# Weight-block sums stored ahead for v and the last gate; the last stage's rows kept in operand tiles, its norm's weights applied before the root

## The chip, the cores and the metric

One Trainium2 chip, one NeuronCore of it. The metric is device time in microseconds of one execution, the median of three runs. All engine times below come from one profiled execution, in which each engine's instructions are recorded; times there count from the start of the span.

## The reference, cut to what matters

A decoder layer on h of shape (1024 tokens, 1024 channels), float32. The parts that the change touches are the projection for v and the last step:

```python
z = rmsnorm(h, mix_pre_g) @ w_in          # 1024 x 5120; columns 1024:2048 are v
v = gelu(z[..., 1024:2048])               # then a layer norm and the spatial gate
...
gate = sigmoid(rmsnorm(h, ple_pre_g) @ ple_w_gate)
e = p @ ple_w_proj
h = h + rmsnorm(gate * e, ple_post_g)     # rmsnorm(y, g) = y * rsqrt(mean(y*y) + 1e-6) * g
```

Ahead of each of the two products stands a feed-forward block, h + 0.5 * rmsnorm((silu(n @ w_gate) * (n @ w_up)) @ w_down), with 2816 hidden channels.

## The kernel before, in words

Every large product is made from seven products of half-sized blocks (a Winograd form of Strassen's scheme). `ORDER` lists them as p1, p2, p5, p6, p3, p7, p4. A float32 operand is split in two float32r parts, high and low: `split` (L147, L148) makes a cast on ScalarE (ACT) and a subtraction on VectorE (DVE). `mm3` (L155 to L157) makes three matmuls of 128x512 from them.

The left operand's seven sums live in seven tiles of the pool X (class `Seven`, one [128, 2, 4, 512] tile for each product; the pool has seven buffers, and an eighth tile, `rest`, holds sums in between). They are made from the normed rows of eight token tiles t = 0 to 7. `closing` computes such a row tile when the product before it ends: the residual (L730), its squares on ACT (L168), the root on GpSimd (POOL; `rsqrt`, L162 and L163), the norm (`scaled`, L178), then `feed`: eight transposes on TensorE (PE; L232) and the sums and splits of the transposed tile (L207, L212, L214, L215, L148). Tiles 4 to 7 come last, and their `late` part feeds p5 and what follows.

The right operand of v and of the last gate is made by class `Rows`: two half tiles (pool wt, four buffers) for each of the seven products, one product ahead of its use. With no stored sums it takes `from_blocks`: p1 and p2 use a block as loaded, p5, p6, p7 and p4 add blocks in place with `each` (L368, recorded at L151), two additions of 128x1024 on DVE for each product. With stored sums (w_out_a, w_out_b and w_o already have them, by `store_sums` during the first feed-forward block's second product) it takes `from_stored`: p1, p2, p3 load a block, the other four load a sum from DRAM, and nothing is added.

`Rows.run` makes four products of 12 matmuls for each entry of `ORDER`, one for each of four row groups. Entry i takes t = 0 to 3; block results are combined by `Out.read` (L333 to L345) and handed to `final`: half 0 of tiles 0 to 3 at p2, half 1 of them at p3, half 1 of tiles 4 to 7 at p7 and half 0 at p4. For v that is `v_final`, for the last stage `ple_final` (L1169): a load of e's half row into a tile of pool hf (four buffers), sigmoid (L1179), the product with e (L1180), squares (L168) and a part of the mean on POOL (L174). A tile's second half also loads h's row into a tile of pool raw (six buffers, shared with the weight loads), takes the root, and for each half scales (L178), adds the row (L151) and stores (L1191).

`Later` holds deferred steps with a key and a cost in us; `allow` pops some after each product, `flush` empties it. In `ffn_hidden` (two calls, 11 groups of columns each) `after(c)` defers the group's sums (`spill`) and `down_sums(c)`, which for one 128-row pair of w_down loads two tiles of pool f (11 buffers), makes four additions of 128x512 and stores four results. All loads and stores but four go through SyncE's (SP's) queue in order. The order on each engine comes from a list scheduler that simulates the program; the program's order is the priority.

Of the kernel before, what the change touches and what calls it, by code (L numbers as in the profile page):

```python
# [8 lines left out]
F32 = mybir.dt.float32  # L9
FR = mybir.dt.float32r  # L10
AF = mybir.ActivationFunctionType
ALU = mybir.AluOpType
# [71 lines left out]
def layer_kernel(ctx: ExitStack, tc: tile.TileContext, a: dict, out: bass.AP):  # L84
# [42 lines left out]
    def scratch(name, n, w=D):  # L127
        return [dr.tile([P, w], F32, name=f"{name}{i}", tag=f"{name}{i}") for i in range(n)]
# [4 lines left out]
    as_d, bs_d = (scratch(s, 7, KD // 2 * HT) for s in ("a_s", "b_s"))  # L133

    tw_d = {s: [scratch(f"{s}_t{h}", 4) for h in range(2)] for s in ("w_out_a", "w_out_b", "w_o")}
    ws_d = dr.tile([P, HT], F32, name="ws_d", tag="ws_d")
# [43 lines left out]
    def gain(vec):  # L180
        g = full()
        nc.sync.dma_start(g, vec.partition_broadcast(P))
        return g
# [5 lines left out]
    class Seven:  # L189
        def __init__(self):  # L190
            self.op, self.kept = [None] * 7, {}
            count[0] += 10
            self.base = count[0]
# [312 lines left out]
    class Rows:  # L506
        def __init__(self, w, stored=None):

# [24 lines left out]

            make = from_stored(block, put, sums) if stored else from_blocks(block, put)
            self.right = Right(lambda i: make(i, state, (False, False)), list(range(7)), 1)

        def run(self, left, outs, last):
            for i, (name, place, fresh) in enumerate(ORDER):
                if i == 6:
                    last()  # L540
                left.need(i)
                o = self.right.get(i)
                for t in range(4):
                    if i == 2:
# [45 lines left out]

    def ffn_hidden(s, left, cols, last):
        wd = a[f"{s}_w_down"][0]
# [38 lines left out]
        def after(c):  # L631
            spill(hid.pop(c), lambda i: s_d[s][i][:, c * HT:(c + 1) * HT])
            if c < HC - 1:
                down_sums(c)
            if c == HC - 2:
                down_sums(c + 1)
            if c == HC - 1:
                later.flush()
# [233 lines left out]

    down = down_weights("ffn1")
    ffn_hidden("ffn1", left, h1_cols, lambda: down.ahead(3))
    v_rows = Rows(w_in[:, D:2 * D])
    left = Seven()
# [279 lines left out]

    down = down_weights("ffn2")
    ffn_hidden("ffn2", left, h2_cols, lambda: down.ahead(3))
    ple_rows = Rows(a["ple_w_gate"][0])
    left = Seven()  # L1160
# [5 lines left out]

    m, parts, gains = {}, {}, []

    def ple_final(t, half_, part):  # L1169
        if not gains:  # L1170
            gains.append(gain(a["ple_post_g"][0]))
        g_ple = gains[0]
        h = slice(half_ * HT, (half_ + 1) * HT)
        if t not in m:
            m[t] = full()
        mt = m[t]
        e = half()
        nc.sync.dma_start(e, e_d[t][:, h])
        nc.scalar.activation(mt[:, h], part, AF.Sigmoid)  # L1179
        nc.vector.tensor_tensor(mt[:, h], mt[:, h], e, op=ALU.mult)  # L1180
        if half_ != (1 if t < 4 else 0):
            parts[t] = mean_part(mt[:, h], e, 1.0 / D, EPS)
            return
        hp = raw([D])
        nc.sync.dma_start(hp, h3_d[t])
        r = rsqrt(squares(mt[:, h], e), 1.0 / D, parts[t])
        for j in range(2):
            hj = slice(j * HT, (j + 1) * HT)
            scaled(mt[:, hj], mt[:, hj], r, g_ple[:, hj])
            add(hp[:, hj], hp[:, hj], mt[:, hj])  # L1190
            nc.sync.dma_start(out[0, t * P:(t + 1) * P, hj], hp[:, hj])  # L1191

    ple_rows.run(left, token_out(ple_final, m), lambda: None)


# [27 lines left out]
```

## Time and profile before

| what | us |
|---|---|
| median of 3 runs | 2148.37 (2146.13 to 2148.41) |
| the profiled execution | 2153.78 |
| its span, first to last instruction | 2151.7 |
| mean granted TensorE clock | 0.983 of full speed |
| PE busy | 2070.9 (96%) |
| DVE busy | 1472.0 (68%) |
| ACT busy | 939.9 (44%) |

Read the shares of busy time as averages over stages. The table of stretches gives the same for each stage, the timelines tell which instruction an idle engine waited for, in square brackets with the idle time ahead of it. A row that merges several instructions has xN at its end.

### The profile page before, as it was taken

Reading aid. Unit: us, or ns where it says so; the run is one execution under the profiler, and the core shown is the slowest. Engines: PE = TensorE matmul, PEld = TensorE weight load, DVE = VectorE, ACT = ScalarE, POOL = GpSimd, SP = SyncE. Lnnn points to the kernel's source line nnn. Section 1 sums busy time; section 2 is a strip of 40 time slices with the busy share of each in tenths; the row PEclk is TensorE's granted clock in tenths of the full one; section 3 lists DMA queues with packets and bytes.
Section 4 is the critical chain, followed back from the end, with each engine's and each line's share of the span. In section 5 each row is a group of like instructions: output and inputs, shape, how many; then the busy total and the mean of one; then the engine's idle time right before and its main releaser. Section 6 shows DMA issues by size and latency. Waiting matters only on the chain. (4 is left out here: it accounts for less than half of the span.)

```text
span 2151.7 us, 25497 instructions
## 1 busy us (share of the span) xinstructions
PE 2070.9 (96%) x9228; PEld 1712.7 (80%) x9228; DVE 1472.0 (68%) x1773; ACT 939.9 (44%) x1360; POOL 141.0 (7%) x212
## 2 busy tenths in 40 slices
PE   7999999999999799999999999989999999999986
PEld 6888888888887688888787887778888888888765
DVE  6866666677566887567576758886666667545687
ACT  7533333344435543334455535643333334444553
POOL 2000000000021110000000002300000000002112
PEclk9999999999999899999999999999999999999988
DMA  8454545399768236445389986635454547764635
GB/s 287 128 171 157 176 142 184 129 340 384 298 221 320 69 100 193 158 142 177 128 282 340 324 233 204 195 112 188 146 186 136 172 149 272 231 197 175 225 118 195
DMA packets 301486, 429.52 MB, mean 200 GB/s; under 512 B 19888, under 2 KB 176560, under 8 KB 301360
## 3 DMA queue, kind: packets, MB, share of 16 engines
q1 hardware_dynamic: 300272, 425.80, 58.3%
q0 software_dynamic: 1088, 2.10, 0.6%
q8 instruction: 72, 1.18, 0.2%
q14 instruction: 54, 0.44, 0.1%
HBM read 290.72 MB, written 137.10 MB: 199 GB/s over the span
## 5 line engine op out<-in xcount | busy, mean ns | idle before, releaser
L155 PE MATMUL ps<-X,wt 128*128 128x512 f32 x1904 | 743.0, 391 | 4.1 <-DVE f L345 2.4
L156 PE MATMUL ps<-X,wt 128*128 128x512 f32 x1904 | 743.2, 390 | 0.9 <-DVE X L148 0.9
L157 PE MATMUL ps<-X,wt 128*128 128x512 f32 x1904 | 741.8, 390 | 0.0
L148 DVE TENSOR_TENSOR wt<-raw,wt 128x1024 fp32r<-128x1024 f32 x282 | 343.5, 1220 | 235.0 <-ACT wt L147 234.9
L155 PEld LDWEIGHTS ps<-X,wt 128*128 128x128 f32 x1904 | 359.3, 189 | 79.3 <-DVE f L345 2.8
L156 PEld LDWEIGHTS ps<-X,wt 128*128 128x128 f32 x1904 | 359.2, 189 | 76.0 <-DVE X L148 1.8
L157 PEld LDWEIGHTS ps<-X,wt 128*128 128x128 f32 x1904 | 358.8, 188 | 74.7
L147 ACT CAST wt<-raw 128x1024 fp32r<-128x1024 f32 x282 | 295.5, 1050 | 268.7 <-PE ps L157 129.2
L148 DVE TENSOR_TENSOR X<-raw,X 128x1024 fp32r<-128x1024 f32 (+1 forms) x201 | 224.0, 1145 | 113.6 <-ACT X L147 113.1
L147 ACT CAST X<-raw 128x1024 fp32r<-128x1024 f32 (+1 forms) x201 | 192.1, 993 | 156.2 <-PE ps L157 66.6
L156 PE MATMUL ps<-X 128*128 128x512 f32 x616 | 241.5, 392 | 0.3 <-DVE X L148 0.3
L155 PE MATMUL ps<-X 128*128 128x512 f32 x616 | 237.4, 391 | 3.7 <-ACT X L147 2.6
L157 PE MATMUL ps<-X 128*128 128x512 f32 x616 | 240.2, 391 | 0.0
L151 DVE TENSOR_TENSOR raw<-raw 128x1024 f32<-128x1024 f32 x136 | 165.8, 1221 | 15.4 <-DMA raw<-in_w_in_dram 5.5
L155 PEld LDWEIGHTS ps<-X 128*128 128x128 f32 x616 | 116.1, 189 | 28.6 <-ACT X L147 3.0
L156 PEld LDWEIGHTS ps<-X 128*128 128x128 f32 x616 | 116.4, 189 | 24.7 <-DVE X L148 0.8
L156 PE MATMUL ps<-wt,X 128*128 128x512 f32 x336 | 133.8, 398 | 1.8 <-DVE wt L148 1.8
L157 PEld LDWEIGHTS ps<-X 128*128 128x128 f32 x616 | 116.4, 189 | 24.0
L155 PE MATMUL ps<-wt,X 128*128 128x512 f32 x336 | 132.1, 401 | 1.2 <-DVE f L345 1.2
L157 PE MATMUL ps<-wt,X 128*128 128x512 f32 x336 | 133.0, 396 | 0.0
L340 ACT ACTIVATE f<-ps 128x512 f32<-128x512 f32 x88 | 52.6, 598 | 122.5 <-PE ps L157 122.3
L338 ACT ACTIVATE f<-ps 128x512 f32<-128x512 f32 x88 | 52.0, 597 | 109.4 <-PE ps L157 109.4
(136 smaller groups left out, 1856.9 us busy)
## 6 DMA issues: line engine op xcount, KB each, us to landing
raw<-ffn_s SPq DMA_DIRECT2D x70, 512.0 KB, 5.2
raw<-in_ffn_w_gate_dram SPq DMA_DIRECT2D x96, 256.0 KB, 3.4
raw<-in_ffn_w_up_dram SPq DMA_DIRECT2D x96, 256.0 KB, 4.1
f<-in_ffn_w_down_dram SPq DMA_DIRECT2D x44, 512.0 KB, 4.6
ffn_s<-hf SPq DMA_DIRECT2D x88, 256.0 KB, 3.4
ffn_t<-hf SPq DMA_DIRECT2D x88, 256.0 KB, 4.3
raw<-ffn_t SPq DMA_DIRECT2D x40, 512.0 KB, 5.2
ffn_s<-f SPq DMA_DIRECT2D x66, 256.0 KB, 2.1
```

The costliest lines, as they stand in the source:

```text
L147: nc.scalar.copy(hi, src)
L148: e.tensor_tensor(lo, src, hi.bitcast(F32), op=ALU.subtract)
L151: e.tensor_tensor(dst, u, v, op=ALU.add)
L155: nc.tensor.matmul(ps, wl[1], wr[0], start=first, stop=False, skip_group_check=True)
L156: nc.tensor.matmul(ps, wl[0], wr[1], start=False, stop=False, skip_group_check=True)
L157: nc.tensor.matmul(ps, wl[0], wr[0], start=False, stop=last, skip_group_check=True)
L338: nc.scalar.activation(at("22"), y, AF.Copy, scale=-1.0)
L340: nc.scalar.activation(at("12"), x, AF.Copy, scale=-1.0)
```

## The change

The weight-block sums for v (columns 1024:2048 of w_in) and for ple_w_gate are made during the two `ffn_hidden` calls and stored in DRAM: after groups 3 to 6, `row_sums` defers a step (key 92) that loads two tiles of pool f (rows k and 512 + k of the matrix, 512 KB each) and, two products later, a step (key 93, cost 2.8) with four additions of 128x512 and four stores. `Rows` for v and for the last gate then always takes `from_stored`.

In the last stage e's rows and h's rows are loaded as whole rows, four to a tile of pool X: e's eight rows and the norm's weights at entry 3 (p6), h's rows 0 to 3 at entry 4 (p3) and 4 to 7 at entry 5 (p7). `ple_final` only applies the sigmoid at once; the rest is a step `gated`, kept in a list until its rows have been asked for. For p2's four halves that is the first call at p3. `gated` multiplies by e, takes the squares (the junk goes to a half tile), then multiplies by the norm's weights while the root is pending; after the root a fused multiply and add (mt * r + h) for each half replaces the scale and the addition.

```diff
--- before.py
+++ after.py
@@ -132,6 +132,7 @@
     ga_d, gb_d, y_d = (dr.tile([P, KD, T], F32, name=s, tag=s) for s in ("ga_d", "gb_d", "y_d"))
     as_d, bs_d = (scratch(s, 7, KD // 2 * HT) for s in ("a_s", "b_s"))
 
+    tr_d = {s: [scratch(f"{s}_t{h}", 4) for h in range(2)] for s in ("w_v", "ple_w_gate")}
     tw_d = {s: [scratch(f"{s}_t{h}", 4) for h in range(2)] for s in ("w_out_a", "w_out_b", "w_o")}
     ws_d = dr.tile([P, HT], F32, name="ws_d", tag="ws_d")
     sv_d = dr.tile([P, KD, T], F32, name="sv_d", tag="sv_d")
@@ -504,7 +505,7 @@
         return [one(t) for t in range(4)]
 
     class Rows:
-        def __init__(self, w, stored=None):
+        def __init__(self, w, stored):
 
             state = {}
 
@@ -531,15 +532,16 @@
                     out.append(o)
                 return out
 
-            make = from_stored(block, put, sums) if stored else from_blocks(block, put)
+            make = from_stored(block, put, sums)
             self.right = Right(lambda i: make(i, state, (False, False)), list(range(7)), 1)
 
-        def run(self, left, outs, last):
+        def run(self, left, outs, last, beside=lambda i: None):
             for i, (name, place, fresh) in enumerate(ORDER):
                 if i == 6:
                     last()
                 left.need(i)
                 o = self.right.get(i)
+                beside(i)
                 for t in range(4):
                     if i == 2:
                         later.flush(t + 6 if t < 3 else None)
@@ -588,7 +590,27 @@
         wg, wu = (a[f"{s}_w_{n}"][0] for n in ("gate", "up"))
         return Columns(HC, lambda c: ((wg, c, c + HC), (wu, c, c + HC)), 2)
 
-    def ffn_hidden(s, left, cols, last):
+    def row_sums(w, dst):
+
+
+        def one(k):
+            tiles = [full((2, HT)) for _ in range(2)]
+            for r, t in enumerate(tiles):
+                rows = w[r * HT + k * P:r * HT + (k + 1) * P, :]
+                nc.sync.dma_start(t, rows.rearrange("p (c f) -> p c f", c=2))
+
+            def sums():
+                b11, b12, b21, b22 = (t[:, c, :] for t in tiles for c in range(2))
+                for d, t, u, v in ((0, b11, b11, b12), (2, b12, b12, b22), (1, b22, b11, b22), (3, b21, b22, b21)):
+                    add(t, u, v)
+                    nc.sync.dma_start(dst[k // 2][d][:, (k % 2) * HT:(k % 2 + 1) * HT], t)
+
+            later.add(93, 2.8, sums, 2)
+
+        return [lambda k=k: later.add(92, 0.0, lambda: one(k)) for k in range(4)]
+
+    def ffn_hidden(s, left, cols, last, beside):
+
         wd = a[f"{s}_w_down"][0]
         hid = {}
 
@@ -630,6 +652,8 @@
 
         def after(c):
             spill(hid.pop(c), lambda i: s_d[s][i][:, c * HT:(c + 1) * HT])
+            if c > 2 and beside:
+                beside.pop(0)()
             if c < HC - 1:
                 down_sums(c)
             if c == HC - 2:
@@ -871,8 +895,8 @@
         return steps
 
     down = down_weights("ffn1")
-    ffn_hidden("ffn1", left, h1_cols, lambda: down.ahead(3))
-    v_rows = Rows(w_in[:, D:2 * D])
+    ffn_hidden("ffn1", left, h1_cols, lambda: down.ahead(3), row_sums(w_in[:, D:2 * D], tr_d["w_v"]))
+    v_rows = Rows(w_in[:, D:2 * D], tr_d["w_v"])
     left = Seven()
     ffn_down(
         down, closing(4.0, lambda t: x[t * P:(t + 1) * P, :], h1_d, "ffn1_post_g", "mix_pre_g", left),
@@ -1155,8 +1179,8 @@
     )
 
     down = down_weights("ffn2")
-    ffn_hidden("ffn2", left, h2_cols, lambda: down.ahead(3))
-    ple_rows = Rows(a["ple_w_gate"][0])
+    ffn_hidden("ffn2", left, h2_cols, lambda: down.ahead(3), row_sums(a["ple_w_gate"][0], tr_d["ple_w_gate"]))
+    ple_rows = Rows(a["ple_w_gate"][0], tr_d["ple_w_gate"])
     left = Seven()
     ffn_down(
         down, closing(4.0, lambda t: h2_d[t], h3_d, "ffn2_post_g", "ple_pre_g", left),
@@ -1164,33 +1188,50 @@
     )
 
 
-    m, parts, gains = {}, {}, []
+    m, parts, gains, e, h = {}, {}, [], {}, {}
+
+    def rows_of(src, dst, ts):
+        tile4 = X([4, D], F32)
+        for n, t in enumerate(ts):
+            dst[t] = tile4[:, n]
+            nc.sync.dma_start(dst[t], src[t])
+
+    def beside(i):
+        if i == 3:
+            gains.append(gain(a["ple_post_g"][0]))
+            rows_of(e_d, e, range(4))
+            rows_of(e_d, e, range(4, 8))
+        if i in (4, 5):
+            rows_of(h3_d, h, range(4 * i - 16, 4 * i - 12))
 
     def ple_final(t, half_, part):
-        if not gains:
-            gains.append(gain(a["ple_post_g"][0]))
-        g_ple = gains[0]
-        h = slice(half_ * HT, (half_ + 1) * HT)
+        cols = slice(half_ * HT, (half_ + 1) * HT)
         if t not in m:
             m[t] = full()
         mt = m[t]
-        e = half()
-        nc.sync.dma_start(e, e_d[t][:, h])
-        nc.scalar.activation(mt[:, h], part, AF.Sigmoid)
-        nc.vector.tensor_tensor(mt[:, h], mt[:, h], e, op=ALU.mult)
-        if half_ != (1 if t < 4 else 0):
-            parts[t] = mean_part(mt[:, h], e, 1.0 / D, EPS)
-            return
-        hp = raw([D])
-        nc.sync.dma_start(hp, h3_d[t])
-        r = rsqrt(squares(mt[:, h], e), 1.0 / D, parts[t])
-        for j in range(2):
-            hj = slice(j * HT, (j + 1) * HT)
-            scaled(mt[:, hj], mt[:, hj], r, g_ple[:, hj])
-            add(hp[:, hj], hp[:, hj], mt[:, hj])
-            nc.sync.dma_start(out[0, t * P:(t + 1) * P, hj], hp[:, hj])
-
-    ple_rows.run(left, token_out(ple_final, m), lambda: None)
+        nc.scalar.activation(mt[:, cols], part, AF.Sigmoid)
+
+        def gated():
+            nc.vector.tensor_tensor(mt[:, cols], mt[:, cols], e[t][:, cols], op=ALU.mult)
+            if half_ != (1 if t < 4 else 0):
+                parts[t] = mean_part(mt[:, cols], half(), 1.0 / D, EPS)
+            else:
+                r = rsqrt(squares(mt[:, cols], half()), 1.0 / D, parts[t])
+            nc.vector.tensor_tensor(mt[:, cols], mt[:, cols], gains[0][:, cols], op=ALU.mult)
+            if half_ != (1 if t < 4 else 0):
+                return
+            for j in range(2):
+                hj = slice(j * HT, (j + 1) * HT)
+                nc.vector.scalar_tensor_tensor(h[t][:, hj], mt[:, hj], r, h[t][:, hj], op0=ALU.mult, op1=ALU.add)
+                nc.sync.dma_start(out[0, t * P:(t + 1) * P, hj], h[t][:, hj])
+
+        gated_steps.append(gated)
+        if e and (t >= 4 or half_ == 0 or len(h) > t):
+            while gated_steps:
+                gated_steps.pop(0)()
+
+    gated_steps = []
+    ple_rows.run(left, token_out(ple_final, m), lambda: None, beside)
 
 
 # ---- launch: one core; inputs and outputs as the reference has them ----
```

## Rows read from the trace of the kernel before

**Rows 1.** From the page: the span, and each engine's busy us, share of the span and instructions.

```profile
span 2151.7 us, 25497 instructions
PE 2070.9 (96%) x9228; PEld 1712.7 (80%) x9228; DVE 1472.0 (68%) x1773; ACT 939.9 (44%) x1360; POOL 141.0 (7%) x212
```

**Rows 2.** The table of stretches: start and end, length, each engine's busy us (instructions), the granted TensorE clock, the DMA engines' mean share, GB/s. In order: most of the first hidden stage, v's stage, the hand-over into the last stage, the rest of its products, and the end.

```profile
60.00:465.00 405.00, 405.00 (x1788) 335.48 (x1787) 275.50 (x334) 152.38 (x202) 0.00 (x0) 1.00 0.51 170
...
690.00:771.00 81.00, 68.07 (x295) 55.69 (x295) 62.14 (x81) 42.23 (x70) 15.90 (x18) 0.92 0.25 79
...
2030.00:2075.00 45.00, 32.59 (x139) 26.08 (x138) 38.81 (x51) 25.44 (x48) 12.69 (x16) 0.85 0.41 141
2075.00:2134.00 59.00, 56.91 (x249) 46.24 (x247) 40.98 (x56) 29.46 (x54) 9.20 (x16) 1.00 0.52 164
2134.00:2151.70 17.70, 0.00 (x0) 0.00 (x0) 12.11 (x19) 2.65 (x7) 4.49 (x6) 0.62 0.36 137
```

**Rows 3.** The timeline of PE in the two hand-overs, the transposes of tiles 5, 6 and 7 alone: start, us, engine, line, operation, out<-in, count, and the idle time ahead with what ended it. First v's, then the last stage's.

```profile
702.57 1.09 PE L232 MATMUL ps<-ident,raw 128*128 128x128 f32 x8 [3.05 <-DVE raw L178]
...
711.71 1.97 PE L232 MATMUL ps<-ident,raw 128*128 128x128 f32 x8 [2.58 <-DVE raw L178]
...
726.45 1.97 PE L232 MATMUL ps<-ident,raw 128*128 128x128 f32 x8 [6.60 <-DVE raw L178]
...
2043.11 1.09 PE L232 MATMUL ps<-ident,raw 128*128 128x128 f32 x8 [1.96 <-DVE raw L178]
...
2052.26 1.27 PE L232 MATMUL ps<-ident,raw 128*128 128x128 f32 x8 [2.59 <-DVE raw L178]
...
2067.60 1.97 PE L232 MATMUL ps<-ident,raw 128*128 128x128 f32 x8 [7.17 <-DVE raw L178]
```

**Rows 4.** The timeline of DVE in the same two hand-overs: the weight additions (L151 raw<-raw 128x1024) and the norms of tiles 5, 6 and 7 (L178), some thirty other rows left out.

```profile
699.49 1.22 DVE L151 TENSOR_TENSOR raw<-raw 128x1024 f32<-128x1024 f32 x1 [4.10 <-DMA raw<-in_w_in_dram]
...
701.23 1.28 DVE L178 SCALAR_TENSOR_TENSOR raw<-f,sc 128x1024 f32<-128x1024 f32 x1
...
710.36 1.30 DVE L178 SCALAR_TENSOR_TENSOR raw<-f,sc 128x1024 f32<-128x1024 f32 x1 [0.72 <-POOL sc L163]
...
719.85 2.35 DVE L151 TENSOR_TENSOR raw<-raw 128x1024 f32<-128x1024 f32 x2
...
725.12 1.27 DVE L178 SCALAR_TENSOR_TENSOR raw<-f,sc 128x1024 f32<-128x1024 f32 x1
...
2040.03 1.23 DVE L151 TENSOR_TENSOR raw<-raw 128x1024 f32<-128x1024 f32 x1 [3.02 <-DMA raw<-in_ple_w_gate_dram]
...
2041.78 1.28 DVE L178 SCALAR_TENSOR_TENSOR raw<-f,sc 128x1024 f32<-128x1024 f32 x1
...
2048.37 1.22 DVE L151 TENSOR_TENSOR raw<-raw 128x1024 f32<-128x1024 f32 x1
...
2050.91 1.30 DVE L178 SCALAR_TENSOR_TENSOR raw<-f,sc 128x1024 f32<-128x1024 f32 x1 [0.72 <-POOL sc L163]
...
2061.01 1.21 DVE L151 TENSOR_TENSOR raw<-raw 128x1024 f32<-128x1024 f32 x1
...
2066.27 1.27 DVE L178 SCALAR_TENSOR_TENSOR raw<-f,sc 128x1024 f32<-128x1024 f32 x1
```

**Rows 5.** The timeline of POOL: the second instruction of tile 5's root in v's and in the last hand-over, the first instruction of tile 6's root in the last hand-over, and that of the first output tile's root at p3.

```profile
696.38 0.55 POOL L163 TENSOR_TENSOR sc<-sc,nhalf 128x1 f32<-128x1 f32 x1
...
2038.01 0.55 POOL L163 TENSOR_TENSOR sc<-sc,nhalf 128x1 f32<-128x1 f32 x1
...
2047.33 2.92 POOL L162 TENSOR_SCALAR sc<-sc 128x1 f32<-128x1 f32 x1 [7.10 <-ACT raw L168]
...
2104.51 0.26 POOL L162 TENSOR_SCALAR sc<-sc 128x1 f32<-128x1 f32 x1 [18.29 <-ACT hf L168]
```

**Rows 6.** The timelines of DVE and PE at the change from p7 to p4.

```profile
2116.51 1.23 DVE L151 TENSOR_TENSOR raw<-raw 128x1024 f32<-128x1024 f32 x1 [0.48 <-DMA raw<-in_ple_w_gate_dram]
...
2122.12 0.50 PE L155 MATMUL ps<-wt,X 128*128 128x512 f32 x1 [1.22 <-DVE f L345]
2123.26 0.49 PE L156 MATMUL ps<-wt,X 128*128 128x512 f32 x1 [0.63 <-DVE wt L148]
```

**Rows 7.** The timelines at the end: the sigmoid and the two scales of the first output tile at p3, then the last matmul, the wait for e, the last stores and the last additions.

```profile
2102.17 0.63 ACT L1179 ACTIVATE f<-f 128x512 f32<-128x512 f32 x1 [1.91 <-DVE f L342]
...
2105.44 1.41 DVE L178 SCALAR_TENSOR_TENSOR f<-f,sc 128x512 f32<-128x512 f32 x2 [0.58 <-POOL sc L163]
...
2133.38 0.39 PE L157 MATMUL ps<-wt,X 128*128 128x512 f32 x1
2135.25 0.69 DVE L1180 TENSOR_TENSOR f<-f,hf 128x512 f32<-128x512 f32 x1 [3.53 <-DMA hf<-e]
...
2141.04 7.87 SPq L1191 DMA_DIRECT2D out_dram<-raw  x8
...
2145.46 3.08 DVE L151 TENSOR_TENSOR raw<-raw,f 128x512 f32<-128x512 f32 x5
```

**Rows 8.** From the stretch 60 to 465 us (hidden stage): one line of its DMA issues (out<-in, queue, count, KB each, median us to landing) and the longest line of the SP queue's waits (us in total, times, longest us).

```profile
f<-in_ffn_w_down_dram SPq DMA_DIRECT2D x22, 512.0 KB, 4.7
...
SPq L563 <- DVE f L627: 141.6, 22, 13.8
```

**Rows 9.** The table of stretches, just after the last stage's last transposes (columns as in Rows 2).

```profile
2067.60:2073.40 5.80, 5.80 (x18) 4.92 (x19) 5.80 (x10) 4.37 (x10) 1.36 (x2) 0.50 0.43 140
```

## The prediction

> **What bounds the kernel now.** I began with the page. PE is busy for 96% of the span, DVE for 68%, ACT for 44% [rows 1]. So only time in which PE idles or runs slowly, and what follows its last matmul, can be won. The table of stretches says where that is [rows 2]. In the hidden stage PE is busy for all of its 405 us, 1788 matmuls at 0.2265 us; nothing can be won there, only lost. In v's stage PE lacks 12.9 of 81 us, in the hand-over into the last stage 12.4 of 45, in the rest of its products 2.1 of 59, and after 2134 us it does nothing for 17.7 us while DVE is busy for 12.1. These four places are where the change works, or can.
>
> PE's timeline in both hand-overs has the same picture: before the transposes of tiles 5, 6 and 7 it waits 3.05, 2.58 and 6.60 us in v's stage and 1.96, 2.59 and 7.17 us in the last, each time for the norm L178 on DVE [rows 3]. Between two sets of transposes stand only 24 matmuls, 24 x 0.2265 = 5.4 us and about 0.8 us for the transposes, while the norms of tiles 5, 6 and 7 follow each other in 9.13 and 14.76 us (v) and in 9.13 and 15.36 us (last) [rows 4]. So DVE's chain sets the pace of the hand-overs. Its rows show weight additions in it, L151 on raw tiles, and the first of them holds DVE, which takes its queue in order, for 4.10 us (v) and 3.02 us (last) while its weights come by DMA [rows 4].
>
> **Part 1: no weight additions in the hand-overs.** An addition costs 2.35 / 2 = 1.18 us [rows 4]. Four lie ahead of tile 7's norm in each hand-over: p5's two and p6's two.
>
> First additions: with them goes the wait. In the last stage DVE stops at 2040.03 - 3.02 = 2037.01; tile 5's root is out of POOL at 2038.01 + 0.55 = 2038.56 [rows 5], so its norm can start at some 2038.8 in place of 2041.78, 3.0 us earlier, not the whole 4.2. In v's stage the stop begins at 695.39, the root is out at 696.38 + 0.55 = 696.93 [rows 5], and the norm starts at some 697.1 in place of 701.23: 4.1 us. PE takes tile 5's transposes when its 24 matmuls are done, some 1 us after the norm; DVE runs on ahead, so what it won is not lost.
>
> Second addition: 1.2 us of the 9.13 us between tiles 5 and 6. POOL's small root operation took 2.92 us at 2047.33, against 0.26 us elsewhere [rows 5]; its record ends with the run of DVE instructions that the addition at 2048.37 lengthens. So root and DVE both come earlier by the one addition; it counts once, 1.2.
>
> Third and fourth: 2.35 us of the 14.76 and 15.36 us between tiles 6 and 7, 2.4. The sum: tile 7's transposes 4.1 + 1.2 + 2.4 = **7.7 us** earlier in v's stage, 3.0 + 1.2 + 2.4 = **6.6 us** earlier in the last. PE still has to wait for them: in v's stage tile 6's would be at 711.71 - 5.3 = 706.4, its work ends at about 713, and tile 7's come at 726.45 - 7.7 = 718.8. The whole 7.7 and 6.6 thus reach PE, and since it still idles some 6 us the clock drop behind it (granted 0.50, that is 1.2 GHz, for 5.8 us [rows 9]) stays as it is. From below, this part is worth nothing if another step of the chain (POOL, or the order) turns out to hold the norms; from above, the whole of the waits ahead of tiles 5 to 7, some 12 us in each stage.
>
> Stored sums need casts and subtractions as before; p5 now loads two tiles and not four. Six raw tiles suffice for p5's and the four rows of the residual, and its loads no longer wait for one to come free. Loaded bytes go up by one block of a megabyte in each stage, at 0.25 and 0.41 DMA share [rows 2]; nothing.
>
> At the change from p7 to p4 PE waits 1.22 + 0.63 us [rows 6]: a weight load that had waited for a raw tile, then an addition, cast and subtraction. Raw tiles no longer hold h's rows and the addition is gone: **1.9 us**.
>
> **Part 2: the end.** The last matmul ends at 2133.38 + 0.39 = 2133.8, the span at 2151.7: 17.9 us. DVE waits 3.53 us for e's row, which had no free tile of the four, and then works off a heap: the last five additions alone are 3.08 us, and eight stores follow each other [rows 7]. With e and h loaded ahead, what must follow the last matmul is one tile's chain. The first tile at p3 shows its length undisturbed: from its sigmoid at 2102.17 through product, squares and root to the end of two scales at 2105.44 + 1.41 = 2106.85, 4.7 us [rows 7]; the fused pair is taken at the price of the scales. From DVE's last end, 2145.46 + 3.08 = 2148.54, to the span's end are 3.2 us of store. That is 7.9 us.
>
> It needs DVE to keep up. A half-row operation costs 3.08 / 5 = 0.62 us [rows 7], an entry of `ORDER` 48 x 0.2265 = 10.9 us on PE. The change does not lower the count: six half operations for a tile before (two products with e, two scales, two additions), six after (two with e, two with the weights, two fused). p3 takes 20 of them with the four reads and two weight subtractions, 12.4 + 2.4 = 14.8 us; p7 12 and two, 9.8; p4 16, 9.9. From 34.5 us against 32.7 about 1.8 us are left over at the end. The four halves of p2 that now wait for e must fit into p6, where DVE is nearly idle (tile 7's sums and two subtractions); e's first tile can use the X buffer of p2's operand, free since p2's end, and the weight loads of p3 stand ahead of e's in SP's queue, those of p7 and p4 ahead of h's. I take 7.9 + 1.8 = 9.7 us in place of 17.9: **8.2 us**.
>
> Here a rule speaks against the change. The row shows what a run of DVE instructions does to POOL's root: 2.92 us and not 0.26 [rows 5]. At p4 all DVE work would be of that kind (the sums come straight from PSUM to ACT), and the product with the norm's weights is put exactly beside the root. The Trainium skill (SBUF — State Buffer, "Who interferes with whom") says that a Vector instruction with two SBUF inputs and a GpSimd instruction that reads SBUF exclude each other for a whole instruction; the row agrees in kind, though the wait spans several instructions. The product is queued while ACT still takes the squares, so I count no wait on the last tile; by the row it would be 2.92 - 0.26 = 2.7 us, which a rival takes up.
>
> **Part 3: what is added.** Eight steps of `row_sums`, each two loads of 512 KB, four additions of 128x512 (2.5 us at 0.62) and four stores, in the hidden stages. The nearest rows are `down_sums`' own: 22 such loads (eleven steps) in a stretch in which PE lost nothing and DVE had 405 - 275.5 = 129 us free, ACT more, the DMA engines half [rows 2, 8]. Cost zero; SP's queue is the cover that hides it. It waited up to 13.8 us for DVE in that stretch without a stall [rows 8]. A step that waits for a free f tile (11 buffers; some ten are live at a group's change with the two new ones) holds up the weight loads behind it, and PE waits for those. Ends of the range: 0, and 5.8 us for each step (below).
>
> **Sum.** 7.7 + 6.6 + 1.9 + 8.2 = 24.4 us. Against its own time: 2153.8 - 24.4 = 2129.4 for a profiled execution, span 2127.3. Against the median, 5.4 us below that execution: 2148.4 - 24.4 = **2124.0 us**.
>
> **The rivals.**
> - *The norms are held by something else* (root, residual's row, a new order of the scheduler) and part 1's 14.3 us in the hand-overs do not come: only 1.9 + 8.2 = 10.1, 2138.3 us. For it: POOL's 2.92 us and the 0.72 us that DVE waited for it. Against: DVE hardly idles otherwise between two norms. Should the end not gain either, it falls within 0.2%.
> - *DVE's backlog moves the end.* If e comes late, p2's four halves (8 x 0.62 = 5.0 us) fall into p3, and the root waits its 2.7 us: the end wins 0.5 and not 8.2, 2131.7 us. For it: SP's queue in order, and PE at 10.9 us for an entry against 14.8 on DVE. Here the rows would not do what they are put there for.
> - *PE fills its wait.* If the scheduler puts p2's last two products ahead of tile 7's transposes, 24 x 0.2265 = 5.4 us more in each stage: 2148.4 - 24.4 - 10.8 = 2113.2 us. It didn't before; simulated with fewer DVE instructions it has less reason to.
> - *Slower: the hidden stages stall.* A step that holds SP's queue for another 13.8 us outlasts weights that are two pairs of products ahead (2 x 5.4 = 10.9): 2.9 us of stall, and 5.8 x 0.5 = 2.9 us at half clock [rows 9], 5.8 for a step, 46.4 for eight: 2148.4 - 24.4 + 46.4 = 2170.4 us. It decides from 24.4 / 8 = 3.1 us for a step. For it: these stages have no other slack than the prefetch. Against: `down_sums` do the same eleven times for nothing.
>
> **How the numbers follow.** Forecast 0.62 (by itself 2117 to 2131: the hand-overs and the end each a third off), norms held 0.15, backlog 0.10, PE fills 0.07, slower 0.06. The range takes in the first four and leaves out the last and the edges: 2112 to 2140. A difference of under 0.2%, 4.3 us, is about what a measurement of this kernel can't tell from no change. Faster by more than that: 0.62 + 0.15 + 0.10 + 0.07, less 0.04 for the case within the second one in which the end gains nothing either, 0.90; same 0.04; slower 0.06.
>
> **What the profile after would show.** Right: no raw<-raw addition on DVE between 690 and 771 us or in the last stage; the waits ahead of tile 5's transposes near zero, tile 6's under 1.5 us, tile 7's still 5 to 7 us; PE without a wait at p4; some 10 us from the last matmul to the end; PE without idle time in the hidden stages. Wrong: a DVE wait for POOL or DMA in the place of the additions, p2's four products with e on DVE only after p3's begin, POOL's root operations of 2 us and more at p4, or PE waiting for subtractions in groups 4 to 8 of a hidden stage.

## The result, and the profile after

| | before | after |
|---|---|---|
| median, us | 2147.25 (2146.08 to 2148.41, 4 runs) | 2127.06 (2126.1 to 2128.71, 4 runs) |
| profiled execution, its span | 2147.39, 2145.3 (second trace, below) | 2126.75, 2125.0 |

The ratio is 0.9907, with a 95% interval of 0.989 to 0.9924: faster by 20.2 us, where the prediction had 24.4 and 2124.0.

The trace of before that the prediction read was of an execution of 2153.78 us. A second trace of the same kernel (experiment `e0_before`) has 2147.39. One difference lies between the two stages that the change touches: a cast on ACT waits 4.04 us for its DMA in the first trace and 2.15 us in the second, and the next wait of PE is 2.39 us long in the first and 0.17 us in the second. From the timelines of ACT, first and second trace:

```profile
1127.73 1.05 ACT L147 CAST X<-raw 128x1024 fp32r<-128x1024 f32 x1 [4.04 <-DMA raw<-a_s]
...
1123.11 1.05 ACT L147 CAST X<-raw 128x1024 fp32r<-128x1024 f32 x1 [2.15 <-DMA raw<-a_s]
```

So after is compared below with the second trace: 2145.3 - 2125.0 = 20.3 us of span, which is the difference of the medians. Lines of after are one higher than before's in the helpers (L149 is the split, L152 addition, L163 and L164 the root, L179 the norm, L233 the transposes), L754 is the residual, L1212 the sigmoid, L1215 the product with e, L1220 that with the weights, L1225 the fused pair.

The page of after, answering [rows 1], and its table of stretches, answering [rows 2] (the last three lines are the hand-over into the last stage, its other products and the end):

```profile
span 2125.0 us, 25592 instructions
PE 2064.4 (97%) x9228; PEld 1707.8 (80%) x9228; DVE 1473.6 (69%) x1789; ACT 939.2 (44%) x1360; POOL 140.4 (7%) x212
```

```profile
60.00:465.00 405.00, 405.00 (x1788) 335.49 (x1787) 283.72 (x347) 151.36 (x201) 0.00 (x0) 1.00 0.56 190
690.00:771.00 81.00, 73.34 (x339) 60.69 (x338) 63.02 (x91) 44.68 (x72) 12.90 (x22) 0.96 0.28 93
2020.00:2065.00 45.00, 37.51 (x171) 30.64 (x170) 39.51 (x54) 29.01 (x55) 11.46 (x17) 0.92 0.67 244
2065.00:2114.00 49.00, 48.89 (x216) 40.18 (x214) 36.38 (x54) 26.43 (x51) 11.92 (x18) 1.00 0.34 130
2114.00:2125.00 11.00, 0.00 (x0) 0.00 (x0) 7.03 (x11) 1.97 (x5) 3.40 (x4) 0.63 0.50 191
```

The hidden stage still has PE busy for all of its 405 us, with DVE at 283.7 where it was 275.5. PE now lacks 7.7 us in v's stage (12.9 before) and 7.5 in the hand-over (12.4), and only 0.1 in the products after it. PE's timeline, the transposes of tiles 5, 6 and 7 in both hand-overs, answering [rows 3]:

```profile
698.70 1.04 PE L233 MATMUL ps<-ident,raw 128*128 128x128 f32 x8
...
706.86 1.09 PE L233 MATMUL ps<-ident,raw 128*128 128x128 f32 x8 [1.67 <-DVE raw L179]
...
718.72 1.97 PE L233 MATMUL ps<-ident,raw 128*128 128x128 f32 x8 [5.29 <-DVE raw L179]
...
2030.88 1.04 PE L233 MATMUL ps<-ident,raw 128*128 128x128 f32 x8
...
2039.24 1.09 PE L233 MATMUL ps<-ident,raw 128*128 128x128 f32 x8 [1.87 <-DVE raw L179]
...
2050.76 1.97 PE L233 MATMUL ps<-ident,raw 128*128 128x128 f32 x8 [4.92 <-DVE raw L179]
```

Tile 5 is taken without a wait, tile 7 still waits some 5 us. Tile 6 waits 1.7 to 1.9 us, more than forecast. Why is read from DVE's timeline in the last hand-over, answering [rows 4]: the norms of tiles 5, 6 and 7 (L179), and between the first two tile 6's residual (L754) with what stands just ahead of it.

```profile
2028.71 1.28 DVE L179 SCALAR_TENSOR_TENSOR raw<-f,sc 128x1024 f32<-128x1024 f32 x1
...
2031.71 0.68 DVE L215 SCALAR_TENSOR_TENSOR f<-f,X 128x512 f32<-128x512 f32 x1
2032.31 0.68 DVE L216 TENSOR_TENSOR f<-f,X 128x512 f32<-128x512 f32 x1
2032.91 0.68 DVE L208 TENSOR_TENSOR X<-ps,X 128x512 f32<-128x512 f32 x1
2033.51 1.27 DVE L754 SCALAR_TENSOR_TENSOR f<-f,sc,raw 128x1024 f32<-128x1024 f32 x1
...
2037.90 1.28 DVE L179 SCALAR_TENSOR_TENSOR raw<-f,sc 128x1024 f32<-128x1024 f32 x1 [0.72 <-POOL sc L164]
...
2049.42 1.28 DVE L179 SCALAR_TENSOR_TENSOR raw<-f,sc 128x1024 f32<-128x1024 f32 x1
```

No weight addition is left there. The second trace of before has the same tile's residual (L730) nearer to the norm ahead of it:

```profile
2035.76 1.28 DVE L178 SCALAR_TENSOR_TENSOR raw<-f,sc 128x1024 f32<-128x1024 f32 x1
...
2038.75 1.28 DVE L730 SCALAR_TENSOR_TENSOR f<-f,sc,raw 128x1024 f32<-128x1024 f32 x1
...
2040.55 0.68 DVE L214 SCALAR_TENSOR_TENSOR f<-f,X 128x512 f32<-128x512 f32 x1
2041.15 0.68 DVE L215 TENSOR_TENSOR f<-f,X 128x512 f32<-128x512 f32 x1
...
2044.89 1.30 DVE L178 SCALAR_TENSOR_TENSOR raw<-f,sc 128x1024 f32<-128x1024 f32 x1 [0.72 <-POOL sc L163]
```

The residual now comes 4.80 us after tile 5's norm, where it came 2.99 us after it. Three half operations more stand ahead of it: two of tile 4's sums (L215 and L216, before's L214 and L215), which stood behind it, and the first of tile 5's (L208). At the end, from the timelines of PE, ACT, DVE and POOL, answering [rows 7]:

```profile
2113.50 0.39 PE L158 MATMUL ps<-wt,X 128*128 128x512 f32 x1
...
2113.93 0.60 ACT L1212 ACTIVATE f<-ps 128x512 f32<-128x512 f32 x1 [2.12 <-PE ps L158]
...
2116.40 0.68 DVE L1215 TENSOR_TENSOR f<-f,X 128x512 f32<-128x512 f32 x1
2117.00 0.68 DVE L1220 TENSOR_TENSOR f<-f 128x512 f32<-128x512 f32 x1
2118.48 1.42 DVE L1225 SCALAR_TENSOR_TENSOR X<-f,sc,X 128x512 f32<-128x512 f32 x2 [0.80 <-POOL sc L164]
2119.82 0.68 DVE L1220 TENSOR_TENSOR f<-f 128x512 f32<-128x512 f32 x1
2120.42 1.40 DVE L1225 SCALAR_TENSOR_TENSOR X<-f,sc,X 128x512 f32<-128x512 f32 x2
...
2107.80 3.70 POOL L175 TENSOR_SCALAR sc<-sc 128x1 f32<-128x1 f32 x2 [1.99 <-ACT hf L169]
...
2116.07 1.74 POOL L163 TENSOR_SCALAR sc<-sc 128x1 f32<-128x1 f32 x1 [2.38 <-ACT hf L169]
...
2118.78 0.86 POOL L164 TENSOR_TENSOR sc<-sc,nhalf 128x1 f32<-128x1 f32 x1
```

The last matmul ends at 2113.89 and the span at 2125.0: 11.1 us. The second trace of before has 18.0, from this matmul's end to 2145.3:

```profile
2126.89 0.39 PE L157 MATMUL ps<-wt,X 128*128 128x512 f32 x1
```
In after tile 7's sigmoid is done at 2114.53, but DVE takes its product with e only at 2116.40. Another tile's fused pair (2118.48) stands between that and tile 7's own (2120.42), and tile 7's power, the last row, leaves POOL only at 2119.64.

### The profile page after: what moved, and what is told of

The parts are those of the page before. It is cut to its first block, busy times and chain, and to the rows that moved or that the text cites. A ratio compares the mean times of both kernels' runs of the same rounds, so it can differ in the third digit from the quotient of the medians.

```text
span 2125.0 us, 25592 instructions
## 1 busy us (share of the span) xinstructions
PE 2064.4 (97%) x9228; PEld 1707.8 (80%) x9228; DVE 1473.6 (69%) x1789; ACT 939.2 (44%) x1360; POOL 140.4 (7%) x212
## 5 line engine op out<-in xcount | busy, mean ns | idle before, releaser
L149 DVE TENSOR_TENSOR wt<-raw,wt 128x1024 fp32r<-128x1024 f32 x282 | 343.9, 1221 | 221.2 <-ACT wt L148 208.2
L149 DVE TENSOR_TENSOR X<-raw,X 128x1024 fp32r<-128x1024 f32 (+1 forms) x201 | 223.9, 1145 | 107.1 <-ACT X L148 106.6
L152 DVE TENSOR_TENSOR raw<-raw 128x1024 f32<-128x1024 f32 x120 | 146.6, 1222 | 8.1 <-DMA raw<-in_ffn_w_up_dram 3.6
```

The source lines that it names most:

```text
L149: e.tensor_tensor(lo, src, hi.bitcast(F32), op=ALU.subtract)
L152: e.tensor_tensor(dst, u, v, op=ALU.add)
```

## The experiments

Each but the first was timed beside the kernel before; times are medians.

**e0_before: the kernel before, traced again.**

> The kernel before, unchanged, for a second trace of it. The theory (each of the three terms is worth what the rows of the first trace gave: hand-overs 14.3, change from p7 to p4 1.9, end 8.2) says nothing new here. The profile of before lay 5.4 us above the median of its runs, and the span after is 26.7 us shorter than that profile's, though the medians differ by 20.2. One theory: the wait of 2.55 us at 1129 us with the slow clock behind it (some 4 us together) was that execution's alone; then this trace lacks it and its span is near 2146. The other: it belongs to the kernel and the change took it away; then it is here again and the span is near 2151.

2147.39 us, span 2145.3; the readings above and below use it. The longer wait of the cast, with PE's behind it, was thus the first execution's, as far as two traces can show.

**The two halves of the change.** `e1_sums_only` is after with the last stage of before put back, from `m, parts, gains` to the end: stored sums alone.

```diff
-    m, parts, gains, e, h = {}, {}, [], {}, {}
+    m, parts, gains = {}, {}, []
...
-    ple_rows.run(left, token_out(ple_final, m), lambda: None, beside)
+    ple_rows.run(left, token_out(ple_final, m), lambda: None)
```

`e2_rows_only` is the reverse, before with the last stage of after and the call of `beside` in `Rows.run`: weight blocks are added as before.

```diff
-    ple_rows.run(left, token_out(ple_final, m), lambda: None)
+    ple_rows.run(left, token_out(ple_final, m), lambda: None, beside)
```

> The stored sums alone; the last stage's rows and root as before. By the theory the hand-overs and the change from p7 to p4 win: 7.7 + 6.6 + 1.9 = 16.2 us at most, 2131 us; with what the trace after showed of the hand-overs (7.1 and 6.7) some 13.8 and part of the 1.9, 2132 to 2134. The rival that the norms are held by something else: under 4 us, above 2143. Whether the last gate's loads still wait for raw tiles that hold h's rows at p4 is open; if so the 1.9 stay out.

> The last stage's rows in X tiles and the norm's weights ahead of the root, with the weight blocks still added in the stage. By the theory the end wins 6.8 to 8.2 us and the change from p7 to p4 loses its wait for a raw tile: 2138 to 2141 us, a span of about 11 us from the last matmul to the end. The rival (DVE's backlog moves the end): the additions put 4.7 us more on DVE in p3 to p4, so that the end wins only 2 to 3 us, 2144 to 2146.

e1: 2130.69 us (2129.81 to 2131.48), ratio 0.9926 (0.9912 to 0.9939), 17.0 us gained, 0.3 more than the expectation had at most. e2: 2133.88 us (2132.98 to 2135.34), ratio 0.9941 (0.9929 to 0.9954), 13.8 gained, more than either theory had. Together that is 30.8 us, but both at once gave 20.2: the halves overlap. In e2 the weight additions of p6 are still made, but DVE's timeline shows them behind tile 7's norm and no longer ahead of it. Why the scheduler put them there is not shown.

```profile
2057.01 1.27 DVE L178 SCALAR_TENSOR_TENSOR raw<-f,sc 128x1024 f32<-128x1024 f32 x1
...
2060.61 2.35 DVE L151 TENSOR_TENSOR raw<-raw 128x1024 f32<-128x1024 f32 x2
```

From the last stage's first transposes of tile 4 to tile 7's are 28.4 us there, 25.9 in e1, 26.3 in after and 32.9 in before: e2 gains 4.5 us of the 6.6 without a stored sum. Both halves lose the wait at p4, and both shorten the end: from 18.0 us to 13.9 (e1), 11.0 (e2), 11.1 (both). The last stage's change alone thus gives the whole of the shorter end, with the weight additions still in it.

**e3_sums_unused: the price of making the sums.** The eight steps run and store; nothing reads them, and all else is as before.

```diff
-    v_rows = Rows(w_in[:, D:2 * D], tr_d["w_v"])
+    v_rows = Rows(w_in[:, D:2 * D])
```

> The sums are made and stored in the hidden stages but not read; all else as before. By the theory their cost is zero: 2147 us within 2, PE without a wait in groups 4 to 8 of either hidden stage. By the rival that SP's queue holds up the weights: up to 5.8 us for each of eight steps, 2155 to 2193.

2149.84 us, ratio 1.0011 (1.0002 to 1.002), 0.8 above the range of the theory: by the interval 0.4 to 4.3 us are lost. PE was busy for 405.00 of the 405 us of the first hidden stage again and for 390.00 of 390 in the second (1430 to 1820 us), and tile 4's transposes in v's hand-over came at 691.09 us (691.35 in the second trace of before), so this is not lost where the steps are. Its trace has longer waits of PE elsewhere: 1.23 us at 1128.15 us (0.17 in the second trace of before), and 2.12 us at p4, where the second trace has 0.76 and the first 1.22 [rows 6]. From PE's timeline:

```profile
2117.74 0.50 PE L156 MATMUL ps<-wt,X 128*128 128x512 f32 x1 [2.12 <-DVE f L346]
```

After has neither of these waits, so the loss seems to belong to this mixture, through the order that the scheduler chose for it; that is argued, not shown.

**e10_steps_twice: the same price, doubled.** After, with each of the eight steps done twice.

```diff
-        return [lambda k=k: later.add(92, 0.0, lambda: one(k)) for k in range(4)]
+        def step(k):
+            for _ in range(2):
+                later.add(92, 0.0, lambda: one(k))
+        return [lambda k=k: step(k) for k in range(4)]
```

> The changed kernel, but each of the eight steps that make and store the sums in the hidden stages is done twice: 16 steps, twice the loads, additions and stores. Tests the prediction's cost of zero and its slower rival. Theory (SP's queue and DVE have slack in these stages): no idle time of PE in the hidden stages, 2127 us, within 2 us. Rival (each step holds the queue long enough that PE waits for weights): up to 5.8 us for each of the eight further steps, from 2130 up to 2173 us.

2127.72 us (2126.75 to 2128.7): the same as after. Its table of stretches and its SP queue's waits, both for 60 to 465 us, answering [rows 2, 8]:

```profile
60.00:465.00 405.00, 405.00 (x1788) 335.37 (x1787) 294.20 (x366) 152.42 (x202) 0.00 (x0) 1.00 0.62 211
```

```profile
SPq L565 <- DVE f L653: 127.9, 22, 13.8
```

DVE takes on another 10.5 us, the DMA engines go from 0.56 to 0.62, SP's longest wait stays 13.8 us, and PE idles nowhere in this stretch or in 1430 to 1820 us of the second hidden stage. The slower rival is refuted with as much again to spare.

**The last stage in its parts.** `e4_weights_after_root` leaves the rows in operand memory, with the weights behind the root as before; `e5_rows_as_before` has the weights ahead of the root, and the rows in the old small tiles. All have the stored sums. First e4's edit, then the core of e5's.

```diff
-            nc.vector.tensor_tensor(mt[:, cols], mt[:, cols], gains[0][:, cols], op=ALU.mult)
...
-                nc.vector.scalar_tensor_tensor(h[t][:, hj], mt[:, hj], r, h[t][:, hj], op0=ALU.mult, op1=ALU.add)
+                scaled(mt[:, hj], mt[:, hj], r, gains[0][:, hj])
+                add(h[t][:, hj], h[t][:, hj], mt[:, hj])
```

```diff
-        tile4 = X([4, D], F32)
...
+        e = half()
+        nc.sync.dma_start(e, e_d[t][:, h])
...
+        hp = raw([D])
+        nc.sync.dma_start(hp, h3_d[t])
```

> The changed kernel, but in the last stage the norm's weights are multiplied in after the root again: a scale by root and weights and an addition of h's half row, two operations a half, in place of one product with the weights ahead of the root and one fused multiply-add. The rows of e and h stay in operand memory. Theory: behind the last tile's root stand four half operations and not two, 2 x 0.65 = 1.3 us more, but the product with the weights (0.6 us) no longer stands ahead of the root's turn on DVE, and two halves a tile fewer run beside POOL's operations: 0.5 to 1.3 us more in the tail (11.1 us becomes 11.6 to 12.4), 2127.6 to 2128.4 us. Rival (the products beside the root are what holds POOL): tail shorter by up to 1.7 us, 2125.4 us.

> The changed kernel with stored sums and with the norm's weights ahead of the root, but the rows of e and h are loaded as in the kernel before: e's halves into the four half tiles, h's rows into raw tiles, one by one. With the run that had the stored sums alone (neither) and the changed kernel (both) it parts the last stage's change in two. Theory: the weights' place is worth about 1 us of the tail's 2.8 between those two (13.9 and 11.1 us) and the rows' place the rest: tail 12.5 to 13.5 us, 2128.8 to 2130 us. Rival (the wait for e's tile is hidden now that DVE comes early): tail as in the changed kernel, 2127 us.

| stored sums with | weights behind the root | weights ahead of the root |
|---|---|---|
| rows in small tiles | e1: 2130.69, end 13.9 | e5: 2127.35 (2126.58 to 2129.2), end 11.4 |
| rows in operand memory | e4: 2129.51 (2128.31 to 2132.39), end 14.0 | after: 2127.06, end 11.1 |

The weights' place is worth 3.3 and 2.5 us (the runs of e4 and of after touch at their edges), the rows' place 1.2 and 0.3, less than the runs of one kernel differ: with the sums stored it can't be measured. So e4 is slower than either theory had, and in e5 the rival's number came. No run parts the two without stored sums. DVE's timeline shows the weights' place at the end, in e4 (weights behind the root, an execution of 2132.39 us), with POOL's root of the last tile:

```profile
2119.62 0.68 DVE L1215 TENSOR_TENSOR f<-f,X 128x512 f32<-128x512 f32 x1
2120.22 1.40 DVE L179 SCALAR_TENSOR_TENSOR f<-f,sc 128x512 f32<-128x512 f32 x2
2121.54 2.48 DVE L152 TENSOR_TENSOR X<-X,f 128x512 f32<-128x512 f32 x4
2124.83 1.41 DVE L179 SCALAR_TENSOR_TENSOR f<-f,sc 128x512 f32<-128x512 f32 x2 [0.80 <-POOL sc L164]
2126.16 1.29 DVE L152 TENSOR_TENSOR X<-X,f 128x512 f32<-128x512 f32 x2
...
2121.21 2.95 POOL L163 TENSOR_SCALAR sc<-sc 128x1 f32<-128x1 f32 x1 [2.98 <-ACT hf L169]
```

From the last tile's product with e to DVE's end are 2127.45 - 2119.62 = 7.83 us, in after 2121.82 - 2116.40 = 5.42: additions that the fused pair saves lie there for more than one tile (six of them in e4). POOL's step for the last root is held there for 2.95 us, to 2124.16, as four of these additions run on DVE to 2124.02; DVE then waits 0.80 us for the power.

**e6_parts_on_vector: is it POOL's hold?** In the last stage the two small steps ahead of the power move to DVE.

```diff
-                parts[t] = mean_part(mt[:, cols], half(), 1.0 / D, EPS)
+                parts[t] = scalar_tile()
+                nc.vector.tensor_scalar(parts[t], squares(mt[:, cols], half()), 1.0 / D, EPS, op0=ALU.mult, op1=ALU.add)
...
-                r = rsqrt(squares(mt[:, cols], half()), 1.0 / D, parts[t])
+                ss, ms, r = squares(mt[:, cols], half()), scalar_tile(), scalar_tile()
+                nc.vector.scalar_tensor_tensor(ms, ss, 1.0 / D, parts[t], op0=ALU.mult, op1=ALU.add)
+                nc.gpsimd.tensor_tensor(r, ms, nhalf, op=ALU.pow)
```

> The changed kernel, but in the last stage the two small steps ahead of the root's power (mean part and addition to it) run on DVE, behind ACT's sum of squares; only the power stays on POOL. Theory (POOL's small operations were held for 3.70 and 1.74 us by DVE's run, so that the roots of tiles 4 and 6 came late and DVE's work heaped up ahead of tile 7's): the holds end, the tail falls from 11.1 us by 1 to 2, to 2125 to 2126 us. Rival: DVE, in order, now waits for ACT's squares (about 1.2 us each) ahead of these steps, and what it wins at POOL it loses there: tail 11 to 13 us, 2127 to 2129 us.

2127.11 us (2125.41 to 2129.04). The 3.70 and 1.74 us are gone, none of POOL's operations from 2085 us on takes over 0.94, but the end is 10.8 us long against 11.1, and DVE now waits for the power itself, three times in its last 10 us:

```profile
2119.21 0.93 POOL L1222 TENSOR_TENSOR sc<-sc,nhalf 128x1 f32<-128x1 f32 x1 [2.27 <-DVE sc L1221]
...
2120.18 1.41 DVE L1228 SCALAR_TENSOR_TENSOR X<-f,sc,X 128x512 f32<-128x512 f32 x2 [0.44 <-POOL sc L1222]
```

The holds are real, but the time is the same without them, as the rival had it: DVE now makes the small steps and waits for the power. What the holds cost by themselves is not shown.

**e7_tile7_later and e9_tile6_later: PE's wait, filled by hand.** PE gets tile 7's transposes two products later (e7), and tile 6's one product later as well (e9).

With `later7` at 2, the edit of e7, and then that of e9:

```diff
-            left.feed(hp, t, t + 2, max(3, t))
+            left.feed(hp, t, t + 2, max(3, t) + (later7 if t == 7 else 0))
```

```diff
-            left.feed(hp, t, t + 2, max(3, t))
+            left.feed(hp, t, t + 2, max(3, t) + (later7 if t == 7 else 1 if t == 6 and later7 else 0))
```

> The changed kernel, but in both hand-overs PE takes tile 7's transposes two products later, so that 48 matmuls and not 24 stand between tile 6's transposes and tile 7's: the prediction's third rival (PE fills its wait) made by hand. In the changed kernel PE waits 5.68 us (v) and 5.31 us (last stage) ahead of tile 7's transposes. Theory (PE waits only for tile 7's norm, and nothing is late behind it): the 24 matmuls fill the wait, 5.3 to 5.4 us in each stage, and the clock drop after it is shorter or gone, up to 2.9 us each: 2116.4 to 2110.6 us. Rival (what comes after tile 7's transposes, its sums on DVE and the next products, was as late as they are): the wait only moves behind the two products, 2125 to 2128 us.

> The kernel with tile 7's transposes two products later (2115.03 us), and tile 6's one product later (12 matmuls, 2.7 us) in both hand-overs. PE still waits about 2 us (start gaps of 2.04 and 2.24 us, of which 0.23 is a matmul's own) ahead of tile 6's transposes there. Theory: 1.8 to 2.0 us in each stage come back, 3.6 to 4.0 us, if DVE's backlog at the end does not take them: 2111 to 2112 us. Rival (DVE's backlog sets the end by now): PE ends 2 to 4 us earlier and the tail grows by nearly as much, 2113.5 to 2115.5 us.

e7: 2115.03 us (2114.74 to 2115.17), ratio 0.985 (0.9836 to 0.9863). e9: 2111.07 us (2110.37 to 2111.78), ratio 0.9827 (0.9812 to 0.9841): 16 us faster than after. PE's timeline in the last hand-over, tiles 6 and 7, first e7, then e9:

```profile
2033.70 1.09 PE L233 MATMUL ps<-ident,raw 128*128 128x128 f32 x8 [1.85 <-DVE raw L179]
...
2045.58 1.03 PE L233 MATMUL ps<-ident,raw 128*128 128x128 f32 x8
```

```profile
2032.54 1.03 PE L233 MATMUL ps<-ident,raw 128*128 128x128 f32 x8
...
2044.32 1.09 PE L233 MATMUL ps<-ident,raw 128*128 128x128 f32 x8 [1.41 <-DVE raw L179]
```

In e7 the wait ahead of tile 7 is gone, 48 matmuls of the products fill it, and the clock is granted in full behind it (1.00 in 690 to 771 and in 2060 to 2101 us). PE ends 12.9 us earlier, but the end grows from 11.1 to 12.4 us. Of the 16.4 us at most in the expectation 12.0 came; e9 is inside its theory's range.

**e8_later_and_vector and e11_all_three: e7 and e9, each with e6's edit.**

> The kernel with tile 7's transposes two products later (2115.03 us) and, in the last stage, the two small steps ahead of the root's power on DVE instead of POOL. With tile 7 later PE ends 12.9 us earlier but the tail grew from 11.1 to 12.4 us, and POOL's small operations are held for 3.94, 4.31 and 1.73 us there. Theory A (the longer tail comes from POOL's holds): the tail falls by 1 to 1.5 us, 2113.5 to 2114 us. Theory B (it is DVE's backlog: 5.4 us less time for the same count of operations): no change or up to 0.5 us more, since eight parts and eight sums of some 0.07 us each come to DVE, 2114.5 to 2115.5 us.

> Both hand-over moves (tile 7 two products later, tile 6 one) together with the small steps ahead of the root on DVE. If theory A of the run with tile 7 later and the steps on DVE holds, and tile 6's waits come back too, 2110 to 2111 us; if DVE's backlog sets the end, 2113 to 2115 us.

2116.27 us (2114.85 to 2117.65) and 2112.27 us (2110.99 to 2113.32), each 1.2 us above the kernel without e6's edit, with ranges that overlap; the ends are 12.4 us (e8, as e7) and 10.9 (e11, 10.5 in e9). e8 lies above both ranges of its expectation, e11 between its two. Theory A falls here too: taking the small steps off POOL does not shorten the end. e9 stays the best version.

## Why the prediction was right, and where it was off

The time from the transposes of tile 4 to the norm of tile 5, from there to tile 6's and to tile 7's, gives part 1's three steps by themselves (second trace of before less after; tile 4's transposes start at 691.35 and 2028.66 us in before, at 692.32 and 2024.49 in after):

| step | forecast v, last | measured v | measured last |
|---|---|---|---|
| first additions and their wait | 4.1, 3.0 | 7.63 - 4.21 = 3.4 | 7.10 - 4.22 = 2.9 |
| second addition | 1.2, 1.2 | 9.14 - 9.00 = 0.1 | 9.13 - 9.19 = -0.1 |
| third and fourth | 2.4, 2.4 | 14.76 - 11.87 = 2.9 | 15.36 - 11.52 = 3.8 |
| sum | 7.7, 6.6 | 6.4 | 6.7 |

**First additions.** Right in kind and in size; tile 5's transposes wait no more. In v's stage DVE stops for 3.46 us in the second trace of before and not for the first's 4.10, which is nearly all of the 0.7 us that is missing.

**Second addition.** This step failed: "root and DVE both come earlier by the one addition". In the last stage POOL's first operation for tile 6 does fall from 2.92 us to 0.78, and from tile 6's residual to its norm it is 2037.90 - 2033.51 = 4.39 us in place of 6.14, 1.75 us less. But the residual comes 4.80 - 2.99 = 1.8 us later behind tile 5's norm, so nothing is left. Between the two norms DVE now does ten half operations of 0.60 us and not eight, and the 1.2 us of those two, both of tile 5's sums, are the 1.14 that the addition took from start to start. In v's stage the residual moved as much, from 3.00 us to 4.80. Why the scheduler put the sums ahead of it is not shown. So tile 6 waits 1.7 to 1.9 us and not under 1.5.

**Third and fourth.** They are worth 2.3 us (two of 1.13 or 1.14 from start to start), and what was done early is missing here: in the last stage eleven half operations stand between the norms of tiles 6 and 7 and not fourteen, 1.8 us. 2.3 + 1.8, less some 0.2 in which DVE waits for a sigmoid, are the 3.8 measured. The last stage's sum thus came out right with two terms of it wrong, which is luck.

**p7 to p4.** PE's waits of 1.15 and 1.14 us from start to start there are gone (1.8 us beyond a matmul's own 0.23 each); from tile 7's transposes to the last matmul it is 2.6 us in all against 1.9, with the stretch at half clock behind tile 7's transposes, which the prediction left as it was, some 0.6 us shorter, after a shorter wait.

**The end.** Forecast 17.9 less 8.2, measured 18.0 less 6.9. The sum missed one term: behind the last matmul came DVE's backlog, 2116.40 - 2114.53 = 1.9 us, forecast 1.8; then tile 7's chain, which took 5.4 us from its product with e where 4.1 were counted (4.7 less the sigmoid's 0.63). Another tile's fused pair of 1.4 us stands ahead of tile 7's in that time; tile 7's power is ready only 0.18 us before this pair ends, so how much of the 1.3 us is the pair's and how much POOL's is not shown. Who earns the 6.9 was told wrong: the prediction gave it to rows "loaded ahead". e1 has 4.1 of it from stored sums alone, e5 6.7 without the rows in operand memory, e4 hardly more than e1 with them. The 3.53-us wait for e's tile looks like a mark of DVE's backlog and not its cause: with the old small tiles it falls to 1.86 us in e1, and in the last 20 us of e5 DVE waits for e once, for 0.49 us. What helped there were the stored sums, with which DVE has two pairs of weight additions less to do beside p3 and p7 (that it is these is argued), and fewer operations behind the root. But e2 has 7.0 of it without a stored sum, and since it moves rows and weights together, what the rows earn without stored sums stays open.

**Hidden stages.** Cost zero, right: e10 shows room for twice as much, and what e3 lost shows no wait of PE in them.

**What was not foreseen.** PE waits for DVE 1.0 us longer than it must behind v's stage, in after and, 0.7 us, in e1. From PE's timeline of after:

```profile
804.97 0.33 PE L156 MATMUL ps<-f,raw 128*128 128x128 f32 x1 [0.83 <-DVE raw L946]
```

v's stage also began 1.0 us later, within the 691.1 to 694.3 of the traces here.

The sum of the account: 6.4 + 6.7 + 2.6 + 6.9, less 1.0 for the later start of v's stage and 1.3 between its last transposes and the last hand-over (the new wait is 1.0 of it), is 20.3. Against the forecast, v's hand-over fell short by 1.3, the end by 1.3, the later start and that stretch took 2.3, and p4 gave 0.7 and the last hand-over 0.1 more: 24.4 - 4.1 = 20.3.

**The rivals.** Norms held by something else: true of tile 6 alone, some 1.2 us in each stage and not 14.3 in all. DVE's backlog: p2's products with e came ahead of p3, and its 1.9 us were in the sum; POOL's holds were there, at 3.70 and 1.74 us, but the time does not fall with the small steps on DVE (e6, e8, e11). PE fills its wait: the scheduler didn't do it, e7 and e9 did by hand, for 12 and 16 us. Hidden stages that stall: refuted by e10.

## What to carry to other kernels

When an operation leaves a chain on an in-order engine, ask what may come ahead of the next link in its place: here sums that had stood behind a residual came ahead of it and took what an addition had freed. A wait for a buffer beside a backlog is often only its mark, so change the operation count and the buffer each alone before crediting either. Where PE waits for one chain, look first for work in its queue that does not depend on it: putting products ahead of the waiting transposes gave 16 us, on top of the 20 of the whole change.

## What the runs showed of the hardware

Two waits that hardly differ were followed by different clocks. In the last hand-over PE idled 1.89 us ahead of tile 6's transposes in e8 (the line below) and 1.85 us in e7 (shown above); in e8 the granted clock then fell to 0.50 (1.2 GHz), in e7 it stayed at 1.00 (2.4 GHz). After e8's line, the table of stretches of 2034.2 to 2037.6 us, e8 and then e7:

```profile
2033.37 1.21 PE L233 MATMUL ps<-ident,raw 128*128 128x128 f32 x8 [1.89 <-DVE raw L179]
```

```profile
2034.20:2037.60 3.40, 3.40 (x11) 2.72 (x10) 3.40 (x5) 1.03 (x2) 1.25 (x1) 0.50 1.01 414
```

```profile
2034.20:2037.60 3.40, 3.40 (x19) 2.87 (x18) 3.40 (x5) 1.18 (x2) 1.51 (x2) 1.00 1.02 418
```

The 48 matmuls behind the transposes take from 2034.23 to 2046.58 us in e8 and from 2034.55 to 2045.35 in e7, by the starts of the first and the last. That is 12.35 and 10.80 us, 1.55 us apart, behind waits that differ by 0.04 us. What decides between the two levels there isn't shown.
